# adaLN by row sums on VectorE, one SSD matrix a head, differential norms inside their cores, parameters a phase earlier

## The chip, the cores and the metric

The kernel runs on one core of a Trainium2 chip. The metric is the device time of one execution in microseconds (us). The engines are TensorE (PE, matmuls; PEld its weight loads), VectorE (DVE), ScalarE (ACT), GpSimd (POOL) and SyncE (SP, which issues most DMAs).

## What is computed

One inference step of a hybrid backbone: 2 layers over 128 context and 512 latent tokens of width 1024, all in fp32. The same weights serve both kinds of tokens, with two conditioning vectors (`c_ctx` and `c`). Of each layer:

```python
sh1, sc1, g1, sh2, sc2, g2 = split(silu(cond) @ w_mod[l] + b_mod[l], 6)   # adaLN: parts 0 to 5
h = rmsnorm(x, g_norm1) * (1 + sc1) + sh1
z, xbc, dt, u, dq, dk, dv, wq, wk, wv = split(h @ w_in)
y_a = ssd_mixer(z, xbc, dt)        # bidirectional Mamba-2, chunks of 128, 8 heads of 64
y_b = s5_mixer(u)                  # bidirectional S5
o = (softmax(q1 k1) - lam * softmax(q2 k2)) v      # differential attention, 4 heads
y_c = rmsnorm(o, subln_g) * (1 - lam_init)
y_d = windowed_attention(wq, wk, wv)
merged = sum_i sigmoid(h @ w_gate_i) * (y_i @ w_branch_i) @ w_out
x = x + g1 * merged
h2 = rmsnorm(x, g_norm2) * (1 + sc2) + sh2
x = x + g2 * (relu(h2 @ w_fc1) ** 2 @ w_fc2)
```

Within a chunk and a head the SSD is, for each direction, y = (C B^T * decay, lower or upper triangle) (dt * x); the two directions are added.

## The kernel before

Activations lie feature-major, `[128, 8, 640]`, each as a rounded part and a remainder (`hh`, `hl`; `nh`, `nl`; `fh`, `fl`; `mh`, `ml`). A dense product is three matmuls for each of 8 slices of depth (`mm3_step`, L223 to L225): 24 matmuls of 320 columns make one group in a `dn` tile of PSUM, of which there are two. Weights come with SP's queue (`wr`), ACT rounds them (`wh`, L212), and DVE, every third time POOL, makes the remainder (`wl`, L196), in rings of 4. A group is emptied from PSUM by its evacuation: in the MLP's first half by ACT's Relu and DVE's product `r` (L1746), then ACT's `fh` and the remainder `fl`; in its second half by DVE's multiply-add into `x` (L1538).

The stages, with their times in the profiled execution: prologue (0 to 45), pre (to 195), mix of layer 0 (to 820, its SSD from 445 to 570), end and output projection (to 1042), MLP of layer 0 (1075 to 1595), then the same for layer 1 (SSD from 1905 to 2040, mix to 2270, MLP from 2560).

The order of the mix is written by hand: PLAN is a string of letters, each of which steps one generator (`c` is `ssd_core`, `a` and `A` are `diff_core` for two heads each, `f` is `diff_finish`, `k` the windowed attention, `q` the merge of the differential branch); a table says which must be whole before another begins. A list scheduler then orders the instructions of each engine statically, by priorities; on the chip each engine runs its own list in order.

**adaLN.** A part of the modulation vectors is 1024 numbers for two conditions. `adaln_ahead` makes a quarter of a part a visit: weights in 256 KB tiles `wa` (a ring of 8), 8 matmuls with the condition (L288), ACT copies the row `mrow` out (L293), two matmuls with a selector turn it into columns (L295), DVE adds the bias (`mod`, L298). In layer 0 parts 0 and 1 are made in the prologue; the other 40 visits come ahead of their use: 12 in pre and the output projection, the other 28 in the MLP of layer 0. There `between`, after each two groups, steps one chain of generators 5 times in 8 turns: the rest of adaLN, the builder of layer 1's S5 tables (`s5_build`, its products `cmul` at L593 to L595 on DVE and POOL), adaLN again.

**SSD.** For a chunk and a group g of four heads: `sseg` (the decay's exponents for two directions, DMA, then DVE and POOL subtract, L1022), their minimum (L1026), the exponential (ACT, L1027); `mf` and `ee` are its products with the masked scores `cm` of the two directions (L1033 on POOL, L1034 on DVE); two matmuls a head (L1037, L1038) with `xd`, which is x times the dt of a direction (POOL, L1006). `y` is evacuated by DVE (L1041).

**Differential branch.** `diff_core` leaves raw outputs in the tiles of its queries (`dq` and `BT`) and their sums of squares in `dss`. `diff_finish` computes one `rsqrt` of 128x20 on DVE (L174 to L186), multiplies (L1467), and `to_branch` transposes on PE (L1127) into the tile `B` that the merge's dense groups read (ACT L1131, DVE L1132).

## Time and profile before

| | us |
|---|---|
| median of 3 runs | 2989.94 (2985.88 to 3001.45) |
| profiled execution, its own time | 2994.21 |
| its span | 2992.4 |
| PE busy in the span | 2831.8 (95%) |
| DVE busy | 1686.3 (56%) |
| ACT busy | 1181.3 (39%) |
| POOL busy | 832.8 (28%) |
| mean granted clock of PE | 0.976 |

The chain of work that ended last runs over PE for 72%, DVE for 13%, DMA for 4%, issue for 3%. The share of an engine is an average over stages that differ; what an instruction is worth is read in its own stage, from what waits for it there. Matmuls overlap, so their durations sum to more than the time they take: the distance of two starts is the cost of one.

### The profile page before, as it was taken

The numbers are of one execution on the slowest core, as the hardware profiler recorded it, in microseconds if no ns is written. First come the engines' busy times: TensorE is split into PE (matmuls) and PEld (weight loads), VectorE is DVE, ScalarE is ACT, GpSimd is POOL, SyncE is SP. The second block draws the span as 40 slices with busy tenths as digits, with TensorE's granted clock in tenths as the row PEclk, the third lists the DMA queues.
The fourth block names the chain that finished last, engine by engine and source line by source line (L and its number), as shares of the span: only waits on it lengthen the run. The fifth ranks groups of instructions, "written<-read, shape, count | busy, mean of one in ns | idle before, by whom it ended". The sixth has DMA issues, their size and how long they took to land.

```text
span 2992.4 us, 53739 instructions
## 1 busy us (share of the span) xinstructions
PE 2831.8 (95%) x20782; PEld 2651.5 (89%) x20782; DVE 1686.3 (56%) x3574; ACT 1181.3 (39%) x2692; POOL 832.8 (28%) x823
## 2 busy tenths in 40 slices
PE   7889998999799999999999999989999999999999
PEld 5878988898689888899998989978997999999999
DVE  7859737665543456646235686576665436433333
ACT  4344563253344242323234555424534434332322
POOL 2743106522212222424111220363131131211111
PEclk9989999998899999999999999989999999999999
DMA  6753343234432635434443433432262323222222
GB/s 225 256 174 112 100 136 102 80 99 136 141 100 75 239 103 174 146 114 159 153 144 112 158 100 115 136 92 66 86 198 86 103 89 106 68 75 78 75 75 85
DMA packets 241855, 364.19 MB, mean 122 GB/s; under 512 B 42272, under 2 KB 104480, under 8 KB 241600
## 3 DMA queue, kind: packets, MB, share of 16 engines
q1 hardware_dynamic: 226848, 336.97, 36.0%
q10 hardware_dynamic: 14752, 23.78, 2.2%
q8 instruction: 164, 2.69, 0.4%
q14 instruction: 91, 0.75, 0.1%
HBM read 294.98 MB, written 65.68 MB: 121 GB/s over the span
## 4 chain that ended last, share of the span: by engine, by line
PE 72%; DVE 13%; DMA 4%; issue 3%; ACT 2%; POOL 2%; SPq 0%; DVEq 0%; ACTq 0%; POOLq 0%
PE dn L223 20%; PE dn L224 20%; PE dn L225 20%; DVE wl L196 2%; DMA sseg<-acum 1%; PE mx L288 1%; PE mx L1278 1%; PE pb L1322 1%; PE mx L1407 1%; PE mx L1452 1%; PE mx L1316 1%; DVE B L767 1%; DVE sc L766 1%; PE mx L743 1%; DVE cv L902 1%
## 5 line engine op out<-in xcount | busy, mean ns | idle before, releaser
L196 POOL TENSOR_TENSOR wl<-wr,wh 128x512 fp32r<-128x512 f32 x207 | 287.1, 1387 | 1340.7 <-ACT wh L212 1254.5
L212 ACT CAST wh<-wr 128x512 fp32r<-128x512 f32 (+1 forms) x614 | 377.3, 620 | 600.5 <-PE dn L224 525.1
L196 DVE TENSOR_TENSOR wl<-wr,wh 128x512 fp32r<-128x512 f32 (+1 forms) x407 | 326.4, 805 | 318.1 <-ACT wh L212 306.4
L223 PE MATMUL dn<-hh,wh 128*128 128x320 f32 x1328 | 422.3, 318 | 12.3 <-ACT us L695 3.8
L224 PE MATMUL dn<-hl,wh 128*128 128x320 f32 x1328 | 420.2, 316 | 2.8 <-DVE hl L401 1.5
L225 PE MATMUL dn<-hh,wl 128*128 128x320 f32 x1328 | 418.8, 316 | 1.6 <-DVE wl L196 1.6
L223 PE MATMUL dn<-nh,wh 128*128 128x320 f32 x992 | 311.1, 314 | 6.6 <-DVE r L1746 6.6
L223 PE MATMUL dn<-fh,wh 128*128 128x320 f32 x1008 | 313.6, 311 | 2.9 <-DVE x L1538 2.9
L224 PE MATMUL dn<-nl,wh 128*128 128x320 f32 x992 | 308.5, 311 | 3.9 <-DVE nl L401 1.6
L225 PE MATMUL dn<-fh,wl 128*128 128x320 f32 x1008 | 312.1, 310 | 0.0
L224 PE MATMUL dn<-fl,wh 128*128 128x320 f32 x1008 | 311.8, 309 | 0.0
L225 PE MATMUL dn<-nh,wl 128*128 128x320 f32 x992 | 307.6, 310 | 0.0
L223 PEld LDWEIGHTS dn<-hh,wh 128*128 128x128 f32 x1328 | 253.4, 191 | 19.4 <-ACT us L695 4.1
L223 PE MATMUL dn<-wh,hh 128*128 128x256 f32 (+1 forms) x880 | 259.2, 296 | 8.2 <-DVE dtraw L1207 3.0
L224 PE MATMUL dn<-wl,hh 128*128 128x256 f32 (+1 forms) x880 | 256.8, 293 | 10.5 <-DVE wl L196 8.5
L224 PEld LDWEIGHTS dn<-hl,wh 128*128 128x128 f32 x1328 | 253.3, 191 | 8.3 <-issue 3.2
L225 PEld LDWEIGHTS dn<-hh,wl 128*128 128x128 f32 x1328 | 253.2, 191 | 6.9 <-issue 3.8
L225 PE MATMUL dn<-wh,hl 128*128 128x256 f32 (+1 forms) x880 | 256.0, 292 | 0.0
L1538 DVE SCALAR_TENSOR_TENSOR x<-dn,mod,x 128x192 f32<-128x192 f32 (+2 forms) x240 | 98.0, 436 | 225.2 <-PE dn L225 217.7
L223 PE MATMUL dn<-B,wh 128*128 128x320 f32 x640 | 206.2, 323 | 12.7 <-ACT B L825 3.4
L224 PE MATMUL dn<-B,wh 128*128 128x320 f32 x640 | 202.1, 316 | 0.2 <-DVE B L196 0.2
L225 PE MATMUL dn<-B,wl 128*128 128x320 f32 x640 | 200.4, 313 | 0.0
(399 smaller groups left out, 6505.6 us busy)
## 6 DMA issues: line engine op xcount, KB each, us to landing
wr<-in_w_fc_dram SPq DMA_DIRECT2D x256, 256.0 KB, 2.8
wa<-in_w_mod_dram SPq DMA_DIRECT2D x160, 256.0 KB, 4.5
wr<-in_w_gate_dram SPq DMA_DIRECT2D x128, 256.0 KB, 2.8
wr<-in_w_tok_dram SPq DMA_DIRECT2D x80, 256.0 KB, 2.9
wr<-in_w_branch_dram SPq DMA_DIRECT2D x64, 256.0 KB, 3.0
acc<-gth SPq DMA_DIRECT2D x48, 320.0 KB, 3.1
gold<-acc SPq DMA_DIRECT2D x48, 320.0 KB, 3.7
gate<-gah ACTq DMA_DIRECT2D x70, 160.0 KB, 1.8
```

Of the source, the lines that this page charges most:

```text
L196: engine.tensor_tensor(out=out, in0=full, in1=hi, op=ALU.subtract)
L212: nc.scalar.copy(out=hi, in_=raw)
L223: nc.tensor.matmul(ps, sh, vh, start=first, stop=False)
L224: nc.tensor.matmul(ps, sh, vl, start=False, stop=False)
L225: nc.tensor.matmul(ps, sl, vh, start=False, stop=last)
L288: nc.tensor.matmul(acc[r0:r0 + 32, i * 256:i * 256 + 256], cpad[:, k, :], raw(part, k // 2)[:, c0:c0 + 256], start=(n_ < 4), stop=(n_ >= 4),)
L743: nc.tensor.matmul(xs[:, ri, g * NI:(g + 1) * NI], pm[:, ri, g * 128:(g + 1) * 128], U[:, g0 + g], start=True, stop=True)
L766: nc.vector.tensor_tensor(out=t, in0=v.to_broadcast(shp), in1=x.to_broadcast(shp), op=ALU.mult)
L767: nc.vector.tensor_tensor(out=dst, in0=dst, in1=t, op=ALU.add)
L902: nc.vector.scalar_tensor_tensor(out=cv, in0=xp[:, k:k + 646], scalar=cw[:, f, k:k + 1], in1=cv, op0=ALU.mult, op1=ALU.add)
L1278: nc.tensor.matmul(sc[:, n, c0:c0 + (k1 - k0) * 128], qT[rows[n], g, ct], kT[rows[n], k0:k1].rearrange("p k c -> p (k c)"), start=True, st ...
L1538: nc.vector.scalar_tensor_tensor(out=xs, in0=ps[:, c0:c1], scalar=mods[l][:, part * 8 + f, s:s + 1], in1=xs, op0=ALU.mult, op1=ALU.add)
```

## The change

1. **adaLN in the MLP stages** is made on DVE. The conditioning vectors are spread over all partitions (`cb`), the weights come transposed, 128 outputs x 1024 inputs a tile of 512 KB (`w_modt`, ring of 3), and one instruction multiplies a tile with a condition, sums along the row and adds the bias. One such row op is issued after each evacuation (`fill`). The visits of the first three parts that were still to come for layer 0 stay on PE, ahead of the MLP; the 28 in MLP 0 go. 96 row ops stand in MLP 0 and 16 in MLP 1. The S5 builder is stepped once in six turns. `cmul`'s temporaries have one buffer there instead of two.
2. **SSD**: `md`, the scores of both directions weighted by dt and added (ACT and DVE, a head at a time), is multiplied with the decay once; one matmul a head, on x itself. `xd` and `mf` go.
3. **Differential branch**: each `diff_core` ends with its own `rsqrt` (128x10) and products; `diff_finish` only transposes.
4. **Small parameters** of a layer (`params`) are prepared in the prologue and at the end of the MLP before.
5. The last layer's final squares are left out, as nothing reads them.

The diff, cut to its core:

```diff
-    t1=3, tx=4, tq=6, ty=2, tw=5, td=5, nt=4, wa=8, wr=4, wh=4, wl=4, fh=10,
+    t1=3, tx=4, tq=6, ty=2, tw=5, td=5, nt=4, wa=3, wr=4, wh=4, wl=4, fh=10,
...
-    sub0="v", sub1="p", mf="p", ef="v", xd="p", xw="p", xD="p", off="p", z="v", qkn="p", qka="p", qkc="v",
+    sub0="v", sub1="p", xw="p", xD="p", off="p", z="v", qkn="p", qka="p", qkc="v",
...
-        return ring("wa", 512, "ada" if "ada" in top else "pool")(shape, name)
+        return ring("wa", 1024, "ada" if "ada" in top else "pool")(shape, name)
...
+    cr = tmp([128, 16], "cr", bufs=1)
+    sp.dma_start(out=cr, in_=a["c_rows"])
+    crt = tmp([128, 16], "crt", bufs=1)
+    nc.scalar.activation(out=crt, in_=cr, func=AF.Tanh, scale=0.5)
+    nc.vector.tensor_scalar(out=crt, in0=crt, scalar1=0.5, scalar2=0.5, op0=ALU.mult, op1=ALU.add)
+    nc.vector.tensor_tensor(out=cr, in0=cr, in1=crt, op=ALU.mult)
+    c_d = dp.tile([128, 16], F32, name="c_d")
+    sp.dma_start(out=c_d, in_=cr)
...
-                    if n not in halves:
-                        halves[n] = wa([128, 512], "wa")
-                        sp.dma_start(
-                            out=halves[n], in_=a["w_mod"][l, part * 4 + q, n // 2][:, (n % 2) * 512:(n % 2) * 512 + 512]
-                        )
-                    return halves[n]
+                    if n // 2 not in halves:
+                        halves[n // 2] = wa([128, 1024], "wa")
+                        sp.dma_start(out=halves[n // 2], in_=a["w_mod"][part * 4 + q, n // 2])
+                    return halves[n // 2][:, (n % 2) * 512:(n % 2) * 512 + 512]
...
+    def cond_rows():
+
+        cb = big([128, 2, D], "cb")
+        sp.dma_start(out=cb.rearrange("p s k -> p (s k)"), in_=c_d.rearrange("a b -> (a b)").unsqueeze(0).to_broadcast((128, 2 * D)))
+        return cb
+
+    def adaln_rows(l, parts, cb, after=()):
+
+        for part in parts:
+            for f in range(part * 8, part * 8 + 8):
+                with tc.high_priority(offset=AHEAD):
+                    w = wa([128, D], "wa")
+                    sp.dma_start(out=w, in_=a["w_modt"][l * 48 + f - 40])
+                prod = mx().rearrange("p a b -> p (a b)")
+                for s in range(2):
+                    nc.vector.tensor_tensor_reduce(
+                        out=prod, in0=w, in1=cb()[:, s], scale=1.0, scalar=bmod[l][:, f:f + 1], op0=ALU.mult,
+                        op1=ALU.add, accum_out=mods[l][:, f, s:s + 1],
+                    )
+                    if s and f % 8 == 7 and part in after:
+                        make_gsc(l, after[part])
+                    yield
 
...
-            u, v = big(shape, "s5u", bufs=2, where=where), big(shape, "s5v", bufs=2, where=where)
+            u, v = (big(shape, t, bufs=2 if where == "build" else 1, where=where) for t in ("s5u", "s5v"))
...
-            xd = [times(dt[:, c, 8 * d:8 * d + 8], "sxd") for d in range(2)]
...
+                md = tx([128, 4, 128], "smd")
+                for h in range(4):
+                    n = 4 * g + h
+                    nc.scalar.activation(out=md[:, h], in_=cm[:, 0, g], func=AF.Copy, scale=dt[:, c, n:n + 1])
+                    nc.vector.scalar_tensor_tensor(
+                        out=md[:, h], in0=cm[:, 1, g], scalar=dt[:, c, 8 + n:9 + n], in1=md[:, h], op0=ALU.mult,
+                        op1=ALU.add,
+                    )
...
-                eng("mf").tensor_tensor(out=mf, in0=ee, in1=cm[:, 1, g].unsqueeze(1).to_broadcast(b4), op=ALU.mult)
-                eng("ef").tensor_tensor(out=ee, in0=ee, in1=cm[:, 0, g].unsqueeze(1).to_broadcast(b4), op=ALU.mult)
+                nc.vector.tensor_tensor(out=ee, in0=ee, in1=md, op=ALU.mult)
                 for h in range(4):
                     hc = slice((4 * g + h) * 64, (4 * g + h) * 64 + 64)
-                    nc.tensor.matmul(yp[:, hc], ee[:, h], xd[0][:, hc], start=True, stop=False)
-                    nc.tensor.matmul(yp[:, hc], mf[:, h], xd[1][:, hc], start=False, stop=True)
+                    nc.tensor.matmul(yp[:, hc], ee[:, h], r["xs"][:, c, hc], start=True, stop=True)
             xw = [times(wd[:, d], "sxw") for d in range(2)]
...
-    def diff_core(l, i, qkv, nlam, ss):
+    def diff_core(l, i, qkv, nlam):
+        ss = tmp([128, NT, 2], "dss")
...
-                yield
-
-    def diff_finish(l, outs, ss, gs, var):
-        rs = rsqrt(ss.rearrange("p i t h -> p (i t h)"), NT * 4, 1.0 / 128)
-        rs = rs.rearrange("p (i t h) -> p i t h", i=2, h=2)
+                if (t, h) != (NT - 1, 1):
+                    yield
+        rs = rsqrt(ss.rearrange("p t h -> p (t h)"), NT * 2, 1.0 / 128).rearrange("p (t h) -> p t h", h=2)
+        for t in range(NT):
+            ov = qT[:, :, t * 128:(t + 1) * 128]
+            eng("diff").tensor_tensor(
+                out=ov, in0=ov, in1=rs[:, t].unsqueeze(2).to_broadcast((128, 2, 128)), op=ALU.mult
+            )
+
+    def diff_finish(l, outs, gs, var):
         yo = var["yc"] = branch_tiles()
         for i in range(2):
             for t in range(NT):
                 ct = slice(t * 128, (t + 1) * 128)
-                ov = outs[i][:, :, ct]
-                eng("diff").tensor_tensor(
-                    out=ov, in0=ov, in1=rs[:, i, t].unsqueeze(2).to_broadcast((128, 2, 128)), op=ALU.mult
-                )
-                to_branch(yo, [ov[:, h] for h in range(2)], t, lambda f: gs[:, 0:1], 2 * i)
+                to_branch(yo, [outs[i][:, h, ct] for h in range(2)], t, lambda f: gs[:, 0:1], 2 * i)
                 yield
...
-            nc.vector.scalar_tensor_tensor(
+            ins = nc.vector.scalar_tensor_tensor(
                 out=xs, in0=ps[:, c0:c1], scalar=mods[l][:, part * 8 + f, s:s + 1], in1=xs, op0=ALU.mult, op1=ALU.add
             )
+        return ins
...
+    def params(l):
+
+        bg = tmp([128, 32], "bgh", bufs=1)
+        sp.dma_start(out=bg, in_=a["b_gate"][l])
+        nc.vector.tensor_scalar(out=bg, in0=bg, scalar1=0.5, scalar2=None, op0=ALU.mult)
+        return bg, qk_gains(l), diff_params(l)
...
+        prm = params(0)
         build_after[0] = h[1][0:1, KT - 1, T - 1:T].bitcast(F32)
-        adgen = adaln_ahead(0, range(2, 6), {4: 1})
+        adgen = adaln_ahead(0, (2, 3, 4), {4: 1})
...
+            rows = iter(())
+
+            def fill(ins):
+
+                with tc.issue_after(ins.ins):
+                    step(rows)
+
             def res(part, squares, f, hf, ps):
-                residual(l, part, ps, hf, f, x)
+                ins = residual(l, part, ps, hf, f, x)
                 if squares:
                     square_into(acc_n, x, f, hf)
+                fill(ins)
 
...
-                nc.vector.tensor_tensor(out=r, in0=r, in1=ps, op=ALU.mult)
+                ins = nc.vector.tensor_tensor(out=r, in0=r, in1=ps, op=ALU.mult)
                 hi, lo = hsl(act[j], 0, hf)
                 nc.scalar.copy(out=hi, in_=r)
                 sub_lo(lo, r, hi)
+                fill(ins)
...
-            bgen = [adgen]
+            cb = cond_rows()
+            step(adgen, 99)
+            rows, bgen = adaln_rows(l, (5,), lambda: cb), iter(())
             if l + 1 < L:
-                bgen += [
-                    adaln_ahead(l + 1, (0, 1), {1: 0}),
-                    s5_build(l + 1, "mlp", lambda: act0[7][1][0:1, 0, T - 1:T].bitcast(F32)),
-                    adaln_ahead(l + 1, range(2, 6), {4: 1}),
-                ]
-            bgen = itertools.chain(*bgen)
+                rows = itertools.chain(rows, adaln_rows(l + 1, range(5), lambda: cb, {1: 0, 4: 1}))
...
-                step(bgen, turn * 5 // 8 - (turn - 1) * 5 // 8)
+                step(bgen, int(turn % 6 == 0))
...
-                        res(5, q == 3, f, hf, ps[:, :HF])
+                        res(5, q == 3 and l + 1 < L, f, hf, ps[:, :HF])
...
+            step(rows, 99)
             if l + 1 < L:
+                prm = params(l + 1)
...
+    p["w_modt"] = np.concatenate([inp["w_mod"][0].T.reshape(48, 128, D)[40:], inp["w_mod"][1].T.reshape(48, 128, D)])
```

**DVE in the first MLP stage, where the S5 tables of layer 1 are built.** Names: `r` and `fl` belong to evacuations, `wl` to weights, the `s5` names to the builder; `ISA` on 128x1024 is a row op and on 128x1 the read of its sum. Before:

```order
L593 TENSOR_TENSOR s5u_14611<-s5pin_14078,s5bt_14593 128x512
L1746 TENSOR_TENSOR r_2544_13483<-r_2544_13483,dn_13458 128x320
L595 TENSOR_TENSOR s5bt_14593<-s5u_14600,s5v_14601 128x64
L593 TENSOR_TENSOR s5u_14616<-s5pin_14078,s5bt_14593 128x512
L196 TENSOR_TENSOR fl_13269<-r_2544_13483,fh_13268 128x320
L196 TENSOR_TENSOR wl_13615<-wr_13612,wh_13614 128x512
L1746 TENSOR_TENSOR r_2546_13513<-r_2546_13513,dn_13488 128x320
L595 TENSOR_TENSOR s5pt_14610<-s5u_14611,s5v_14612 128x512
```

In the changed kernel:

```order
L1797 TENSOR_TENSOR r_2586_13595<-r_2586_13595,dn_13570 128x320
L352 ISA mx_13602,mod_102<-wa_13600,cb_12212,bmod_98 128x1024
L352 ISA mod_102 128x1
L626 TENSOR_TENSOR s5pt_13810<-s5u_13816,s5v_13817 128x512
L196 TENSOR_TENSOR wl_13715<-wr_13712,wh_13714 128x512
L196 TENSOR_TENSOR fl_13393<-r_2586_13595,fh_13392 128x320
L624 TENSOR_TENSOR s5u_13838<-s5pou_12802,s5c_13791 128x512
L1797 TENSOR_TENSOR r_2590_13629<-r_2590_13629,dn_13604 128x320
L352 ISA mx_13602,mod_102<-wa_13600,cb_12212,bmod_98 128x1024
```

Each evacuation (`r`, now L1797) is followed by a row op and its read, ahead of the builder's and the weights' operations; the builder's stand further apart.

**PE at the end of the mix of layer 0.** `dn` are dense groups, `pa<-ident,dq` and `pa<-ident,BT` the transposes of the two halves of the differential outputs, L1278 and L1316 (now L1315 and L1353) the windowed attention. Before:

```order
L225 MATMUL dn_8659<-B_7376,wl_8602 128x320
L1278 MATMUL mx_8949<-wkT_1579,xs_7391 128x128 x2
L1127 MATMUL pa_8701<-ident,dq_534_2488 128x128 x2
L1127 MATMUL pa_8709<-ident,dq_534_2488 128x128 x2
L1316 MATMUL mx_8968<-ident,wp_8957 128x128
...
L1127 MATMUL pa_8717<-ident,dq_534_2488 128x128 x2
L223 MATMUL dn_8796<-B_8699,wh_8782 128x320
```

In the changed kernel:

```order
L225 MATMUL dn_8551<-B_7418,wl_8509 128x320
L1164 MATMUL pa_8761<-ident,dq_527_2479 128x128 x2
...
L225 MATMUL dn_8598<-B_7418,wl_8585 128x320
L1164 MATMUL pa_8768<-ident,dq_527_2479 128x128 x2
L223 MATMUL dn_8613<-B_7418,wh_8584 128x320
...
L225 MATMUL dn_8833<-B_8746,wl_8820 128x320
L1164 MATMUL pa_8782<-ident,BT_5979 128x128 x2
L1353 MATMUL mx_9005<-ident,wp_8994 128x128
L1315 MATMUL mx_9014<-wkT_1578,xs_7433 128x128 x2
```

The five transposes of `dq` stood together behind the last dense group of a merge; now each stands alone, with dense groups before and behind it, and the first of `BT` follows dense matmuls too.

**DVE in the SSD of layer 1.** Names as in the section on the kernel; `smd` is `md`. Before:

```order
L1022 TENSOR_TENSOR sseg_20958<-sseg_20958,dac_20919 128x512
L1026 TENSOR_TENSOR sseg_20958<-sseg_20958,sseg_20959 128x512
L1022 TENSOR_TENSOR sseg_20980<-sseg_20980,dac_20919 128x512
L1029 TENSOR_TENSOR swd_20957<-sseg_20958,dtd_20910 128x4 x2
L1022 TENSOR_TENSOR sseg_21214<-sseg_21214,dac_20919 128x512
L196 TENSOR_TENSOR wl_21972<-wr_21969,wh_21971 128x512
L1034 TENSOR_TENSOR sseg_20958<-sseg_20958,scb_20943 128x512
L1026 TENSOR_TENSOR sseg_20980<-sseg_20980,sseg_20981 128x512
```

In the changed kernel:

```order
L1053 SCALAR_TENSOR_TENSOR smd_20949<-scb_20938,dtd_20570,smd_20949 128x128 x3
...
L1053 SCALAR_TENSOR_TENSOR smd_20949<-scb_20938,dtd_20570,smd_20949 128x128
L1061 TENSOR_TENSOR sseg_21059<-sseg_21059,dac_20579 128x512
...
L1072 TENSOR_TENSOR sseg_20958<-sseg_20958,smd_20949 128x512
L1065 TENSOR_TENSOR sseg_21033<-sseg_21033,sseg_21034 128x512
...
L1068 TENSOR_TENSOR swd_21023<-sseg_21033,dtd_20570 128x4 x2
L1072 TENSOR_TENSOR sseg_20984<-sseg_20984,smd_20975 128x512
```

The four multiply-adds of a group stand ahead of the one product (L1034 before, L1072 now) on which PE waits.

## Rows read from the trace of the kernel before

**Rows 1.** Stages: busy us (instructions) of PE, PEld, DVE, ACT, POOL; clock; DMA share.

```profile
445.00:570.00 125.00, 112.52 (x753) 100.32 (x753) 88.82 (x153) 37.83 (x91) 78.23 (x65) 0.93 0.34 97
1075.00:1595.00 520.00, 506.90 (x3910) 471.48 (x3910) 261.50 (x534) 156.04 (x322) 143.64 (x131) 1.00 0.44 143
1905.00:2040.00 135.00, 119.41 (x813) 106.59 (x812) 98.83 (x154) 39.10 (x95) 81.42 (x68) 0.92 0.37 106
2560.00:2992.40 432.40, 428.55 (x2922) 428.28 (x2920) 146.50 (x286) 130.38 (x251) 69.21 (x60) 1.00 0.25 76
```

**Rows 2.** Groups by line, PE, 1075 to 1595: busy, mean, idle before, releaser.

```profile
L288 PE MATMUL mx<-wa,cpad 128*32 128x256 f32 x432 | 33.1, 384 | 2.8 <-DMA wa<-in_w_mod_dram 2.8
...
L295 PE MATMUL mx<-sel,mrow 128*128 128x2 f32 x112 | 14.1, 234 | 0.0
```

**Rows 3.** Timeline of PE around one adaLN visit: start, duration, line, operation.

```profile
1440.67 0.50 PE L295 MATMUL mx<-sel,mrow 128*128 128x2 f32 x4
1441.10 1.07 PE L288 MATMUL mx<-wa,cpad 128*32 128x256 f32 x16
1442.11 0.41 PE L224 MATMUL dn<-fl,wh 128*128 128x320 f32 x1
1442.36 0.31 PE L225 MATMUL dn<-fh,wl 128*128 128x320 f32 x1
```

**Rows 4.** Groups by line and shape over the whole run, DVE and ACT.

```profile
L1291 DVE TENSOR_REDUCE wm<-mx 128x2 f32<-128x1024 f32 x16 | 19.6, 1225 | 41.2 <-PE mx L1285 41.1
...
L1132 DVE SCALAR_TENSOR_TENSOR B<-pa,dgs,B 128x128 fp32r<-128x128 f32 x40 | 13.8, 346 | 6.0 <-ACT B L1131 5.3
...
L1430 ACT ACTIVATION_READ_ACCUMULATOR dp<-mx,dnm 128x1 f32 x80 | 15.7, 197 | 0.0
```

**Rows 5.** Table of 40-us slices of the first MLP stage.

```profile
1280.00:1320.00 40.00, 40.00 (x305) 36.79 (x304) 21.11 (x40) 8.99 (x16) 12.80 (x11) 1.00 0.43 136
...
1360.00:1400.00 40.00, 37.04 (x333) 35.69 (x331) 33.93 (x53) 15.81 (x35) 20.19 (x17) 1.00 0.46 154
```

**Rows 6.** Groups by line: PE in 445:570 and in 1905:2040, POOL in 445:570.

```profile
L1037 PE MATMUL mx<-sxd,sseg 128*128 128x64 f32 x80 | 16.5, 290 | 4.5 <-DVE sseg L1034 4.5
...
L1037 PE MATMUL mx<-sxd,sseg 128*128 128x64 f32 x80 | 16.9, 296 | 5.8 <-DVE ry L186 3.0 <-DVE sseg L1034 2.9
...
L1033 POOL TENSOR_TENSOR sseg<-sseg,scb 128x512 f32<-128x512 f32 x10 | 14.3, 1430 | 9.2 <-ACT sseg L1027 6.7 <-ACT dcl L1021 1.4 <-DMA gate<-gah 1.1
```

**Rows 7.** Timeline in the SSD of layer 0: POOL, DVE, then PE.

```profile
459.85 1.65 POOL L1033 TENSOR_TENSOR sseg<-sseg,scb 128x512 f32<-128x512 f32 x1
...
460.27 1.77 DVE L1022 TENSOR_TENSOR sseg<-sseg,dac 128x512 f32<-128x512 f32 x1
...
462.12 0.68 DVE L1026 TENSOR_TENSOR sseg<-sseg,sseg 128x512 f32<-128x512 f32 x1
...
464.18 0.41 PE L1037 MATMUL mx<-sxd,sseg 128*128 128x64 f32 x2 [0.98 <-DVE sseg L1034]
465.77 0.39 PE L1038 MATMUL mx<-sxd,sseg 128*128 128x64 f32 x2
```

**Rows 8.** Tables of slices: the end of mixing, layer 0 twice, then layer 1.

```profile
765.00:785.00 20.00, 11.51 (x46) 7.42 (x47) 13.69 (x53) 7.43 (x32) 1.67 (x2) 0.51 0.37 122
785.00:800.00 15.00, 11.86 (x71) 7.86 (x69) 9.54 (x31) 7.93 (x28) 0.99 (x2) 0.86 0.00 0
...
2240.00:2280.00 40.00, 36.12 (x254) 29.09 (x255) 26.05 (x79) 22.76 (x74) 6.22 (x6) 1.00 0.22 67
```

**Rows 9.** Timelines of DVE and of PE at 767 to 773.

```profile
767.56 1.76 DVE L1467 TENSOR_TENSOR dq<-dq,ry 128x256 f32<-128x256 f32 x5
...
768.04 0.69 PE L1127 MATMUL pa<-ident,dq 128*128 128x128 f32 x2 [4.67 <-DVE dq L1467]
772.71 0.69 PE L1127 MATMUL pa<-ident,dq 128*128 128x128 f32 x2 [3.98 <-DVE B L1132]
```

**Rows 10.** DMA issues: count, KB each, median us from issue to landing.

```profile
wm<-in_w_mod_dram SPq DMA_DIRECT2D x16, 512.0 KB, 8.4
```

More of the change, by code (lines that the diff above doesn't have):

```diff
@@ L1454, in diff_core @@
                 nc.scalar.activation(
-                    out=pt[:, T:T + 128], in_=po, func=AF.Square, scale=rc[:, 0:1], accum_out=ss[:, i, t, h:h + 1]
+                    out=pt[:, T:T + 128], in_=po, func=AF.Square, scale=rc[:, 0:1], accum_out=ss[:, t, h:h + 1]
                 )
-                yield
-    def diff_finish(l, outs, ss, gs, var):
-        rs = rsqrt(ss.rearrange("p i t h -> p (i t h)"), NT * 4, 1.0 / 128)
-        rs = rs.rearrange("p (i t h) -> p i t h", i=2, h=2)
+                if (t, h) != (NT - 1, 1):
[7 more added lines that the diff above has]
+    def diff_finish(l, outs, gs, var):
         yo = var["yc"] = branch_tiles()
@@ L1575, in panel_adaln @@
                 for i in range(2):
-                    sp.dma_start(out=w[part][i], in_=a["w_mod"][0, part * 4 + q, i])
+                    sp.dma_start(out=w[part][i], in_=a["w_mod"][part * 4 + q, i])
             if soon:
@@ L1621, in hybrid_body @@
             top["pool"] = pool
-            bg = tmp([128, 32], "bgh", bufs=1)
-            sp.dma_start(out=bg, in_=a["b_gate"][l])
-            nc.vector.tensor_scalar(out=bg, in0=bg, scalar1=0.5, scalar2=None, op0=ALU.mult)
+            bg, g, (nlam, gs) = prm
             done, var, sr = {}, {}, {}
@@ L1627, in hybrid_body @@
             y_d = dp.tile([512, 8, NI], F32, name=f"y_d{l}")
-            g = qk_gains(l)
-            nlam, gs = diff_params(l)
-            dss = tmp([128, 2, NT, 2], "dss", bufs=1)
             def glu():
@@ L1651, in hybrid_body @@
                 p=lambda: diff_project(l, 0, h, g, var),
-                a=lambda: diff_core(l, 0, var["qkv", 0], nlam, dss),
+                a=lambda: diff_core(l, 0, var["qkv", 0], nlam),
                 x=lambda: ssd_project(l, h, sr),
@@ L1658, in hybrid_body @@
                 P=lambda: diff_project(l, 1, h, g, var),
-                A=lambda: diff_core(l, 1, var["qkv", 1], nlam, dss),
+                A=lambda: diff_core(l, 1, var["qkv", 1], nlam),
                 z=lambda: ssd_finish(l, sr["xs"], h, var),
@@ L1662, in hybrid_body @@
                 n=lambda: merge(l, 0, h, var["ya"], acc_d, bg, done),
-                f=lambda: diff_finish(l, (var["qkv", 0][0], var["qkv", 1][0]), dss, gs, var),
+                f=lambda: diff_finish(l, (var["qkv", 0][0], var["qkv", 1][0]), gs, var),
                 k=lambda: win_core(l, var["wv"], var["wq"], var["wk"], var),
@@ L1763, in hybrid_body @@
             norm(l, 1, x, acc_n, *h2, PLAN["mid"], tail, head)
-            bgen = [adgen]
+            cb = cond_rows()
+            step(adgen, 99)
+            rows, bgen = adaln_rows(l, (5,), lambda: cb), iter(())
             if l + 1 < L:
-                bgen += [
-                    adaln_ahead(l + 1, (0, 1), {1: 0}),
-                    s5_build(l + 1, "mlp", lambda: act0[7][1][0:1, 0, T - 1:T].bitcast(F32)),
-                    adaln_ahead(l + 1, range(2, 6), {4: 1}),
-                ]
-            bgen = itertools.chain(*bgen)
+                rows = itertools.chain(rows, adaln_rows(l + 1, range(5), lambda: cb, {1: 0, 4: 1}))
+                bgen = s5_build(l + 1, "mlp", lambda: act0[7][1][0:1, 0, T - 1:T].bitcast(F32))
             acc_n = big([128, T], "acc_n")
@@ L1846, in _pack @@
     p["c_t"] = np.stack([_col(inp["c_ctx"]), _col(inp["c"][0])], -1)
+    p["c_rows"] = np.stack([inp["c_ctx"], inp["c"][0]]).reshape(128, 16)
+    w = inp["w_mod"][0].reshape(2, 4, 128, 24, 256)
     p["w_mod"] = st([
-        st([
-            w.reshape(2, 4, 128, 24, 256)[s, :, :, q].transpose(1, 0, 2).reshape(128, 1024) for q in range(24) for s in range(2)
-        ]).reshape(24, 2, 128, 1024) for w in inp["w_mod"]
-    ])
+        w[s, :, :, q].transpose(1, 0, 2).reshape(128, 1024) for q in range(20) for s in range(2)
+    ]).reshape(20, 2, 128, 1024)
+    p["w_modt"] = np.concatenate([inp["w_mod"][0].T.reshape(48, 128, D)[40:], inp["w_mod"][1].T.reshape(48, 128, D)])
     p["b_mod"] = _col(inp["b_mod"])
```

## The prediction

> **What bounds the kernel now.** I read the table of stages first. TensorE (PE) is busy 95% of the span on the page, and in the two MLP stages it runs at the full granted clock: 506.90 of 520 us in the first, 428.55 of 432.4 in the second [rows 1]. Both run the same dense code; the first has 988 more PE instructions (3910 against 2922), of which 432 and 112 are adaLN's [rows 1, 2]. The rest, some 440, build the tables of the next layer's S5 and stay. So in MLP 0 an instruction taken off PE is time, as long as the engines that empty PSUM keep up. VectorE (DVE) is busy only 261.50 of 520 us there [rows 1]. The two stretches with the SSD (445 to 570 and 1905 to 2040) have PE at 112.52 of 125 and 119.41 of 135 and a clock of 0.93 and 0.92, with DVE at 89 and 99 us and POOL at 78 and 81 [rows 1]: there a chain over several engines shares the bound with PE. Last comes the end of layer 0's mixing, where PE from 765 to 785 is busy 11.51 of 20 us at a clock of 0.51 [rows 8].
>
> **Row sums.** Removed from MLP 0 are 27 visits of 16 records at L288 and 28 of 4 records at L295 [rows 2]. What a visit costs is the hole that it leaves in the dense stream, whose matmuls else start 0.147 us apart. Here L295 starts at 1440.67, L288 at 1441.10, the next dense one at 1442.11, and the one behind it 0.25 later instead of 0.147 [rows 3]: 1.44 + 0.10 = 1.54 us for a visit with its L295, 43.1 us for 28. L288 also waited 2.8 us for its weights [rows 2]. Gone: 46 us.
>
> Added to DVE are 96 row ops in MLP 0 (and 16 in MLP 1, where DVE has 146.50 of 432.4 us [rows 1]: nothing). The trace has no such op. The nearest rows are a reduce over 1024 elements of 1225 ns, and the read of an accumulator of 197 ns on ACT [rows 4]; after's order shows two instructions for each row op. I take 1.42 us; 96 x 1.42 = 136 us. DVE then has 261.5 + 136 = 398 of about 487 us, 82%. From below the bound is 1.2 us, the reduce alone, from above 2.85, when the op also waits out a whole POOL op of 1.43 us [rows 6]; I stay at 1.42, since the reduce has the row op's length.
>
> What is queued behind a row op on DVE is the next evacuation, `wl` and the S5 builder's ops. PE takes 24 x 0.147 = 3.5 us for a group of dense matmuls and `dn` has two buffers, so an evacuation that is 1.4 us late is hidden. Where the S5 builder's ops stand between, it isn't always: of the 40-us slices, 1280 to 1320 has DVE 21.11 busy and PE 40.00, 1360 to 1400 has DVE 33.93 and PE 37.04 [rows 5]. With row ops such a load lasts longer: the builder is now stepped once in six turns over the whole stage, and with these durations after's order gives DVE 3.1 to 3.3 us of work for each 3.5 to 3.9 us of PE in some 65 intervals, 250 us in all. At the loss of the slice above (3 of 40 us) that is 19 us; I add 4 for the rest of the stage, so 23 us of stalls. Before there were 520 - 506.9 = 13.1, of which 2.8 are counted above: 12.7 more. Net: -46 + 13 = **-33**. Ends: -46 (stalls stay as they are) and -20 (a loss of 7.5% over all of the stage, 36 us). The rows' weights come as 512 KB a tile, one for two evacuations, the same bytes as before; the ring is a little shallower. DMA share in MLP 0 is 0.44 [rows 1], so I cost that at nothing, and price its failure below (D).
>
> **One SSD matrix a head.** 16 matmuls a chunk become 8. The eight rows of one group of four heads, each one matmul in two records, start from 464.18 to 465.77 [rows 7]: 1.59/7 = 0.227 us apart, and 0.2225 in the rows between. 8 x 5 chunks x 2 layers x 0.2225 = 17.8 us off PE. Off POOL go 10 `mf` of 1430 ns a layer [rows 6] and 10 `xd` of the same size, some 28 us. On DVE come 40 multiply-adds of 128x128, at 346 ns [rows 4] 13.8 us a layer, and on ACT 40 scalings. DVE's `sseg` and `ry` are what PE waited for at L1037, 4.5 us in layer 0 and 5.8 in layer 1 [rows 6]. Against that, DVE ops were stretched while POOL ran: a `sseg` of 1.77 us ended when POOL's `mf` had ended, and the next one of the same size took 0.68 [rows 7]; four of POOL's nine two-input ops a chunk go. The `md` don't hang on the exponential and can run before it; behind it one product is left, without the POOL op in the chain. I take 5 us off the waits: **-23** for both layers. Ends: -12 (of the 27.6 us more on DVE 6 reach PE) and -33 (the 10.3 us of L1037's waits go, and a little clock).
>
> **Differential norms.** In layer 0 a DVE chain (the norm, then ten products, the first five 1.76 us) holds back the first transposes: PE waits 4.67 us for `dq`, then 3.98 on the next link, and the clock falls to 0.51 for 765 to 785 [rows 8, 9]. Idle from 765 to 800 are 8.5 + 3.1 us; the 11.51 busy us at 0.51 are half lost (5.6), and of the 11.86 at 0.86 another 1.7 [rows 8]: 18.9 us. In after's order the five `dq` transposes stand one by one with 20 or more dense matmuls between them, so that stall goes. What is late next are the `BT` ones: between the last product of attention and the first of them stand 43 dense matmuls, 6.3 us, for a norm and 1.76 us of products which took some 9 us before. So 2 to 3 us stay, and the windowed attention's chain behind it, now with more dense matmuls between its links. I take 14 of 18.9. Layer 1's end lost 3.9 us of 40 at full clock [rows 8]; I take 2. **-16**; ends -6 and -23.
>
> **The rest.** The prologue gets one load, one tanh, two small DVE ops and a store on SP's queue ahead of the weights: two issues, up to +1 us. The parameters' preparation had no PE wait behind it, and moves under dense work; if that cover failed it would cost 1 to 2 us. The last layer's squares went beside PE. Together **+1**.
>
> Sum: -33 - 23 - 16 + 1 = -71. The profiled execution took 2994.2 us, 4.3 more than the median of the runs shown, so the result is 2923 by the one and 2919 by the other; I say **2920**.
>
> **Rivals.** (A) DVE becomes the bound of MLP 0. Without row ops it has 261.5 us there, PE has 474: it decides from (474 - 261.5)/96 = 2.2 us a row op. For it: the row op reads two SBUF tensors, and two-input ops of DVE and POOL exclude each other in the trace, 1.77 against 0.68 us [rows 7]. Against it: POOL is busy 144 of 520 us [rows 1], so most row ops meet none. If every one met one: 261.5 + 96 x 2.85 = 535 us, 15 more than now, and the sum is 15 - 38 = -23: 2971. If two in three did, 2.37 us: 489 us and 10 of losses in the chain, 499, -21 - 38: 2935. Say 2950.
> The Trainium skill, page "SBUF — State Buffer", section "SBUF: two separate sides", speaks against the change here: a VectorE op with two SBUF inputs and a GpSimd op that reads SBUF take a shared port pair for their whole duration, and the later one blocks. The rows of 1.77 and 0.68 us agree with it; by that rule, with a collision each time, the time would be rival A's 2971.
>
> (B) The SSD gains nothing: DVE's 13.8 us a layer lie on its chain (`md`, product, `y`), and the matmuls that are left wait as long as those removed took. For it: DVE is at 71 to 73% there [rows 1], and PE's waits name it. Against it: POOL's ops and their collisions go. 2920 + 23 = 2943.
>
> (C) All goes well: stalls stay as before, the waits at L1037 and all of the loss at the end of mixing go: -46 - 33 - 23 + 1 = -101, 2891.
>
> (D) Slower: row ops wait for their weights, with evacuations queued behind them in order. A 512 KB load took 8.4 us at the start, where the queues are full [rows 10], and a tile is used up in 7 to 8 us; with three tiles it is hidden unless loads stand in SP's queue behind others. The other terms give -38, so MLP 0 would have to grow by 38, to 558 us: (558 - 261.5)/96 = 3.1 us a row op, 1.7 of it waiting each time. At 3.6 us it is 607 us, 2994 + 87 - 38 = 3043. The DMA share of 0.44 speaks against.
>
> (E) The change doesn't do what it says at the differential norms: the transposes start earlier and the same stall comes back at `BT`. 2920 + 12 = 2932, inside the forecast's own spread.
>
> **How the numbers follow.** Chances: forecast with E 0.52 (2905 to 2940), A 0.16, B 0.13, C 0.14, D 0.05. The range takes in C's end and most of A: all low ends together give 2891, all high ones -20 - 12 - 6 + 1 = -37, 2957 by the profiled time and 2953 by the median. I set 2888 to 2957; beyond are D and A's upper end. 0.5%, about what a measurement here can tell from no change, is 15 us: 2975 to 3005. Only mixtures of A with B and D reach it. Faster 0.91, same 0.05, slower 0.04.
>
> **What would show it.** In the profile after: MLP 0 near 487 us, no L288 in it, DVE near 80% busy, row ops near 1.2 us with a 0.2 us read; if they are above 2.2, A holds. PE waits on `r`, `x` and `wl` in it between 15 and 30 us. SSD stretches 10 to 13 us shorter each, POOL near 50 us busy there. The waits of 4.67 and 3.98 us on `dq` gone, the clock above 0.85 in the 40 us around the differential transposes. Wrong it would be if evacuations wait for row weights on DVE, or if the SSD's products wait for `smd`.

## The result, and the profile after

The changed kernel takes 2913.7 us (median of 4 runs, 2913.2 to 2917.3) where the kernel before takes 2991.7 (2985.9 to 3001.5): a ratio of 0.9739, 95% interval 0.9711 to 0.9766, or 78 us less. The forecast was 2920, with 2888 to 2957 around it. The profiled execution has a span of 2911.4 us, 81 less than before. The first row below answers to the first of [rows 1], the third to the second, the fourth to the third, the last to the fourth; the second is the end of layer 0's mix, to be held against [rows 8]. Columns as there: stretch, PE, PEld, DVE, ACT, POOL busy, clock, DMA share, GB/s.

```profile
443.00:582.00 139.00, 129.50 (x916) 117.12 (x916) 112.48 (x253) 61.76 (x165) 70.88 (x66) 0.96 0.34 102
735.00:798.00 63.00, 57.07 (x379) 47.98 (x378) 35.43 (x113) 25.56 (x83) 17.81 (x18) 0.92 0.47 154
1025.60:1554.20 528.60, 499.99 (x3555) 480.75 (x3553) 408.90 (x777) 163.47 (x335) 164.10 (x137) 0.98 0.44 140
1845.00:1994.00 149.00, 135.16 (x975) 122.76 (x973) 114.61 (x256) 63.12 (x170) 70.90 (x63) 0.95 0.39 111
2452.50:2911.40 458.90, 451.45 (x3089) 449.09 (x3088) 182.31 (x360) 140.10 (x276) 81.46 (x69) 1.00 0.25 81
```

PE no longer fills the first MLP stage: 28.6 us of 528.6 are idle, and the clock is 0.98 there. DVE rose to 77% of it. POOL's work in the SSD fell by a quarter: from 86.1 to 62.9 us from the 600th to the 800th dense start in layer 0, counted as below.

To place the gain I count PE's dense work. Every kernel here starts 5168 matmuls at L223 (or the line that it has become), so the time from the k-th to another one is the same dense work, whatever lies between. From the timelines of PE, in us:

| from the k-th to the k-th start | before | after | gain |
|---|---|---|---|
| 0 to 600 (pre, first of mix 0) | 410.3 | 404.9 | 5.4 |
| 600 to 1100 (SSD of layer 0 and behind) | 304.6 | 287.7 | 16.9 |
| 1100 to 1600 (end of mix 0, output projection) | 331.9 | 318.3 | 13.6 |
| 1600 to 2600 (MLP 0) | 539.6 | 514.3 | 25.3 |
| 2600 to 3300 (mix 1 with its SSD) | 435.7 | 418.8 | 16.9 |
| 3300 to 4200 (rest of mix 1, output projection) | 499.3 | 497.9 | 1.4 |
| 4200 to the last (MLP 1) | 425.6 | 422.5 | 3.1 |

Each column is one execution. The changed kernel, run once more (f0 below), differs from its column by up to 3.8 us in the first two stretches (291.5 from the 600th to the 1100th start) and by 0.2 or less in the others, so differences of a few us in the first two tell little.

In MLP 0, PE waits as follows (waits of PE, 1025.6 to 1554.2: who for whom, us in total, times, longest):

```profile
PE dn L223 <- DVE r L1797: 15.0, 10, 2.8
PE pb L664 <- DVE s5pt L626: 4.8, 5, 1.6
PE dn L223 <- DVE x L1577: 4.3, 4, 1.3
PE pb L691 <- DVE s5qt L626: 1.1, 1, 1.1
```

In the same view of the kernel before (1075 to 1595) the waits for the evacuations are shorter:

```profile
PE dn L223 <- DVE r L1746: 7.2, 7, 1.4
PE dn L223 <- DVE x L1538: 2.9, 2, 2.2
```

And a wait is there now that the kernel before did not show: PE's transposes of the S5 builder (L664) wait for DVE. DVE is not late because row ops are dear (instructions of line L352: duration min/median/max in ns, first and last start):

```profile
L352 DVE CUSTOM_DVE_ANT_0 mx<-wa,cb,bmod x112: 1272/1284/2262, 1062.0 to 2537.8; 128x1024 f32<-128x1024 f32 x112
L352 DVE DVE_READ_ACCUMULATOR2_ANT mod<- x112: 128/138/144, 1063.2 to 2539.0; 128x1 f32 x112
```

1.28 + 0.14 = 1.42 us for most, and no idle time in front of one. But they are not spread against the builder. Of the slices of 10 us in this stage, those from 1105 to 1275 have DVE busy for 9.7 us or more, all 17; three of them, and one from later:

```profile
1155.00:1165.00 10.00, 7.19 (x49) 6.62 (x47) 9.93 (x11) 2.32 (x5) 8.49 (x6) 1.00 0.46 157
...
1225.00:1235.00 10.00, 7.06 (x47) 6.26 (x45) 9.97 (x19) 1.95 (x5) 3.38 (x4) 1.00 0.40 122
1265.00:1275.00 10.00, 7.64 (x51) 7.13 (x49) 9.77 (x20) 1.86 (x3) 3.63 (x4) 1.00 0.58 203
1375.00:1385.00 10.00, 10.00 (x71) 9.99 (x70) 7.38 (x13) 2.45 (x4) 1.29 (x1) 1.00 0.68 222
```

And late in the stage the builder's matmuls stand between dense ones, one pair at a time (timeline of PE: start, duration, line):

```profile
1429.99 0.41 PE L224 MATMUL dn<-fl,wh 128*128 128x320 f32 x1
1430.33 0.38 PE L691 MATMUL pb<-s5qt,s5bz 128*32 128x112 f32 x2
1430.64 0.41 PE L225 MATMUL dn<-fh,wl 128*128 128x320 f32 x1
...
1442.36 0.47 PE L224 MATMUL dn<-nl,wh 128*128 128x320 f32 x1
1442.63 0.47 PE L225 MATMUL dn<-nh,wl 128*128 128x320 f32 x1
```

A dense matmul and two records of the builder's take 0.65 us, where the dense one alone takes 0.147. This goes on from 1425 to 1439. From 1436.6 the granted clock is at its lower level, 1.2 GHz, for 6.8 us (0.66 over 1435 to 1445), though PE shows no idle time there, and dense matmuls start 0.27 us apart. The clock is also at this level for 3.4 us each from 1235 and from 1314; in the MLP of the kernel before it was not, from 1069 to 1618.

### The profile page after: what moved, and what is told of

Same layout as the page of the kernel before. It is cut to its first block, busy times and chain, and to the rows that moved or that the text cites. A ratio compares the mean times of both kernels' runs of the same rounds, so it can differ in the third digit from the quotient of the medians.

```text
span 2911.4 us, 52387 instructions
## 1 busy us (share of the span) xinstructions
PE 2756.1 (95%) x20062; PEld 2604.5 (89%) x20062; DVE 1817.3 (62%) x3862; ACT 1187.2 (41%) x2729; POOL 799.0 (27%) x783
## 4 chain that ended last, share of the span: by engine, by line
PE 47%; DVE 6%; DMA 1%; issue 1%; ACT 1%; POOL 1%; SPq 0%; ACTq 0%; DVEq 0%; POOLq 0%
PE dn L223 14%; PE dn L224 14%; PE dn L225 14%; DMA sseg<-acum 1%; DVE wl L196 1%; PE mx L1445 1%; PE mx L1315 1%; PE pb L1359 1%; PE mx L1490 1%; PE mx L1353 0%; PE mx L774 0%; DVE mx L352 0%; DVE nh L420 0%; DVE smd L1053 0%; DVE s5u L624 0%
## 5 line engine op out<-in xcount | busy, mean ns | idle before, releaser
L196 POOL TENSOR_TENSOR wl<-wr,wh 128x512 fp32r<-128x512 f32 x207 | 293.8, 1420 | 1299.7 <-ACT wh L212 1249.3
L196 DVE TENSOR_TENSOR wl<-wr,wh 128x512 fp32r<-128x512 f32 (+1 forms) x407 | 314.0, 775 | 241.3 <-ACT wh L212 236.8
L223 PE MATMUL dn<-hh,wh 128*128 128x320 f32 x1328 | 419.9, 316 | 2.8 <-ACT sg L873 0.8
L223 PE MATMUL dn<-nh,wh 128*128 128x320 f32 x992 | 310.9, 314 | 13.2 <-DVE r L1797 12.3
L223 PE MATMUL dn<-fh,wh 128*128 128x320 f32 x1008 | 313.4, 311 | 5.6 <-DVE x L1577 3.4
L223 PE MATMUL dn<-wh,hh 128*128 128x256 f32 (+1 forms) x880 | 258.5, 296 | 5.0 <-ACT hsq L1222 2.3
L223 PEld LDWEIGHTS dn<-hh,wh 128*128 128x128 f32 x1328 | 251.5, 189 | 9.2 <-issue 2.5
L223 PE MATMUL dn<-B,wh 128*128 128x320 f32 x640 | 206.5, 324 | 13.5 <-DVE gth L1556 4.5
L223 PEld LDWEIGHTS dn<-nh,wh 128*128 128x128 f32 x992 | 188.3, 190 | 17.4 <-DVE r L1797 14.5
```

Source lines behind the costliest of these rows:

```text
L196: engine.tensor_tensor(out=out, in0=full, in1=hi, op=ALU.subtract)
L223: nc.tensor.matmul(ps, sh, vh, start=first, stop=False)
```

## The experiments

Theory: each part acts where its instructions are, and what MLP 0 fell short by is DVE, full while row ops and builder meet. Rivals: the parts help each other; row ops are too dear wherever they stand; the SSD's gain is its chain and not its matmuls.

**One part at a time.** e1 has the row sums alone, e2 the SSD, e3 the norms, g4 the parameters; e4 is the changed kernel with adaLN back on PE. Their edits are the pieces of the diff above; e1 has the last layer's squares left out, too.

> The kernel before with the row sums alone (tiles, ring, S5 stepping and the last layer's squares as in the changed kernel). Theory, additive: MLP 0 goes from 551 us (first dense group of the MLP to the first of the next projection) to 528, some 4 us are lost in the output projection of layer 1, where row weights now compete with the loads of x: 18 to 23 us below before, near 2970. By the prediction's own term, -33, it would be 2959. Rival, the gain of the MLP is an interplay with the other parts: less than 10 us below before.

> The kernel before with one SSD matrix a head alone. Theory: 17.8 us of matmuls and some 12 us of waits and half clock go, 30 us below before, near 2962. By the prediction's term, -23, 2969. Rival B (DVE's 27.6 us more eat the gain): less than 8 us below before, 2984 or more.

> The kernel before with the differential norms in their cores alone. Theory: 14 us in layer 0 and 3 in layer 1, near 2975. Rival E (the same stall comes back at the second half's transposes): 2985 or more, with PE waiting there for the products.

> The changed kernel with adaLN back on TensorE; SSD, differential norms and parameters as changed. Theory, additive: 2914 + 20 = 2934 (2930 to 2938); with the prediction's term 2947. Rival, interplay: within 8 us of the changed kernel.

> The kernel before with the small parameters prepared a phase ahead, alone. By the prediction nothing: within 3 us of before. Rival: the three other parts alone give 49 us of the 78, and the changed kernel without row sums is 15 us better than SSD and norms alone, so this part brings 10 us or more, in the first 400 us or after the MLP of layer 0.

| kernel | us | before, beside it | ratio, 95% interval |
|---|---|---|---|
| e1 row sums alone | 2983.5 | 2995.2 | 0.9956 (0.994 to 0.9972) |
| e2 SSD alone | 2972.3 | 2995.2 | 0.9912 (0.9887 to 0.9937) |
| e3 norms alone | 2980.7 | 2995.2 | 0.9945 (0.9927 to 0.9963) |
| g4 parameters alone | 3008.3 | 2996.4 | 1.0034 (1.0019 to 1.005) |
| e4 all but the row sums | 2942.5 | 2995.2 | 0.982 (0.9796 to 0.9845) |

The single parts sum to -12 - 23 - 14 + 12 = -37 us, and all together bring 78: additivity falls. e4 is 26 us above f0 (2917.0, below), between the theory's 20 and the prediction's 33, so its rival falls. e1 with 12 us misses its theory's 18 to 23, though MLP 0 gives what it said. The same count of dense starts shows where (us, gain against before; minus is a loss):

| stretch | e1 | e2 | e3 | g4 | sum | after |
|---|---|---|---|---|---|---|
| 0 to 600 | 2.2 | -0.2 | -3.0 | 0.5 | -0.5 | 5.4 |
| 600 to 1100 | -5.7 | 15.8 | 4.6 | -5.3 | 9.3 | 16.9 |
| 1100 to 1600 | 1.1 | -4.6 | 13.1 | -0.3 | 9.4 | 13.6 |
| 1600 to 2600 | 25.4 | 0.3 | 0.3 | 0.7 | 26.6 | 25.3 |
| 2600 to 3300 | -8.4 | 10.1 | -0.2 | -0.5 | 0.9 | 16.9 |
| 3300 to 4200 | -4.3 | -2.9 | 1.3 | -2.5 | -8.4 | 1.4 |

In MLP 0 the row sums bring the same 25 us alone and in company; e4 has 537.9 there. The norms bring 13.1 in their own stretch, alone and (13.6) in company. What doesn't add lies in the two mixes. e1 edits no instruction of a mix and yet loses 6 us in the first and 13 from the 2600th start to the 4200th. The order in which the list scheduler puts the mix is another one in e1. I wrote down PE's operations from the 100th to the 1600th start by the tiles that they use, neighbours with the same tiles counted once: of 4582 before, 693 have no partner in the same order in e1. The order is the only difference that I found there, but no run changes the order alone, so that it is the cause stays an inference. In the changed kernel 73 of 83 us of gain lie in the four stretches of its main edits, from the 600th to the 3300th start; it is the single parts that lose elsewhere, 37 us being left of 80. So a single part's time carries 5 to 20 us that belong to no edit of it, of which up to 4 us a stretch can be the one execution's own. Rival E falls: in e3 PE's long waits on `dq` are gone and none comes at `BT`. g4 shows that the parameters' gain which I suspected behind e4 isn't there. It is 12 us slower than before, so the "nothing" that it was held against failed, too; what makes it slower is open.

**What a row op costs, and where.** g1 makes every row op twice; f1 ties the S5 builder's steps behind the evacuation at which they are stepped; f2 makes layer 1's last part in MLP 0 too; f3 is f1 and f2; f0 is the changed kernel again.

```diff
 # g1
-                    nc.vector.tensor_tensor_reduce(
+                    for _ in range(2):
+                        nc.vector.tensor_tensor_reduce(
 # f1
-                step(bgen, int(turn % 6 == 0))
+                if turn % 6 == 0:
+                    with tc.issue_after(last[0].ins):
+                        step(bgen)
 # f2
-            rows, bgen = adaln_rows(l, (5,), lambda: cb), iter(())
+            rows, bgen = iter(()), iter(())
...
-                rows = itertools.chain(rows, adaln_rows(l + 1, range(5), lambda: cb, {1: 0, 4: 1}))
+                rows = itertools.chain(adaln_rows(l, (5,), lambda: cb), adaln_rows(l + 1, range(6), lambda: cb, {1: 0, 4: 1}))
```

> The changed kernel with every row op made twice. Theory, DVE decides in MLP 0 from 2.2 us a row op: 96 x 1.6 = 150 us more on DVE, which then has some 555 us where PE has 490, so the stage grows by 45 to 60 us, near 2965. Rival, DVE's slack still covers it: under 15 us.

g1: 2966.1 us, ratio 0.9895 (0.9864 to 0.9925), 49 more than the changed kernel; from the 1600th to the 2600th start 555.1 us instead of 514.3, with DVE busy for 527.4 of them. The stage grows by 41 us, a little under the theory's 45 to 60, and the rest of the 49 lies in the stages behind it. PE waits for evacuations all along (waits of PE, 1040 to 1620), and the row op is no longer than before (1281 ns at the median).

```profile
PE dn L223 <- DVE r L1798: 47.8, 28, 3.5
PE dn L223 <- DVE x L1578: 12.7, 14, 3.0
```

> The changed kernel once more, as the measure for the three beside it: ratio to before near 0.974.

> The changed kernel with the S5 builder's steps tied behind the evacuation at which they are stepped (as the row ops are), so that its blocks are really spread over MLP 0. Theory: the changed kernel's MLP 0 lost its 10 us to a stretch of 170 us in which DVE had row ops and the builder at once and was full; spread, no 10 us have DVE over 95% for long, PE's waits on r, x, s5pt and s5qt fall from 25 us to under 12, and the time falls by 8 us (3 to 15) against the changed kernel. Rival: the row op's length alone makes the waits, wherever the builder stands: within 3 us of the changed kernel, the waits as before.

> The changed kernel with layer 1's last part of adaLN also in MLP 0 (112 row ops there, none and no conditioning load in MLP 1). Theory: the 2.3 us that PE waits for x in layer 1's output projection, with all DMA engines busy there, and the half clock behind it go: 3 to 4 us below the changed kernel; MLP 0 loses at most 2. Rival: the wait is the load of x itself: no difference.

> Both: 11 us below the changed kernel if they add (8 and 3), near 2903.

| kernel | us | before, beside it | ratio, 95% interval | MLP 0 |
|---|---|---|---|---|
| f0 changed kernel | 2917.0 | 2996.0 | 0.9737 (0.9723 to 0.9752) | 514.5 |
| f1 builder spread | 2893.3 | 2996.0 | 0.9666 (0.9645 to 0.9687) | 489.6 |
| f2 last part early | 2915.3 | 2996.0 | 0.973 (0.9715 to 0.9745) | 516.6 |
| f3 both | 2896.7 | 2996.0 | 0.9684 (0.9659 to 0.9708) | 500.7 |

f1 is 24 us faster than the changed kernel and the fastest here; three times what I expected, and a third of it is what I named. DVE is still full from 1105 to 1165, but behind that never for more than 30 us (slices of 10 us with 9.7 us or more). PE's waits (1025.6 to 1530):

```profile
PE dn L223 <- DVE r L1799: 8.9, 11, 1.6
PE pb L664 <- DVE s5pt L626: 4.2, 4, 1.3
PE pb L691 <- DVE s5qt L626: 2.6, 2, 1.6
PE dn L223 <- DVE x L1577: 1.5, 3, 0.7
```

The four kinds fall from 25.2 to 17.2, 8 us; under 12 was expected. The rest is in the holes that the builder's matmuls leave in the dense stream. I measured each as the distance of the dense starts around it, less 0.147. Before, the holes of MLP 0 sum to 85.3 us in 104 places: 39.2 adaLN alone, 26.8 the builder alone, 12.7 with both, 6.7 the norm; longer gaps between dense matmuls add 14.3. After: 46.4 the builder in 64 places, 5.6 the norm, 22.5 the gaps. In f1: 22.9 the builder in 24 places, 6.1 the norm, 20.8 the gaps. So f1 leaves the dense gaps nearly as they were and takes 23.5 us from the builder, 10 of them waits. The clock is in these sums: the 13.7 us that the changed kernel spends at 1.2 GHz in this stage ahead of 1554 are gone in f1, worth some 7 us by an estimate from half speed. The others are the pieces: here one table's matmuls stand together (timeline of PE, f1), 48 records in 1.25 us from dense start to dense start, against 0.65 us for two records when they alternate.

```profile
1166.69 0.31 PE L224 MATMUL dn<-nl,wh 128*128 128x320 f32 x1
1166.93 0.97 PE L691 MATMUL pb<-s5qt,s5bz 128*32 128x112 f32 x32
1167.72 0.23 PE L697 MATMUL pb<-s5c,s5bz 128*32 128x16 f32 x8
1167.78 0.23 PE L697 MATMUL pb<-s5nc,s5bz 128*32 128x16 f32 x8
1167.94 0.41 PE L225 MATMUL dn<-nh,wl 128*128 128x320 f32 x1
```

f2: its mechanism is there. In the output projection of layer 1 (4000th to 4050th start) the changed kernel takes 26.0 us (25.3 in f0), f2 22.0, as before. In the changed kernel's table of slices all DMA engines are busy at that place, with x and row weights at once:

```profile
2395.00:2400.00 5.00, 2.68 (x17) 2.44 (x16) 2.52 (x5) 1.99 (x4) 0.00 (x0) 0.91 1.03 394
2400.00:2405.00 5.00, 5.00 (x28) 5.00 (x28) 0.41 (x2) 0.18 (x1) 0.00 (x0) 0.75 1.03 392
```

But with 16 more row ops MLP 0 is 2.1 us longer in f2 than in f0, and 11.1 us longer in f3 than in f1. So f2 wins 1.7 us, less than the intervals tell apart, and f3 nothing against f1. In f3 most of the loss is clock: MLP 0 has 24 us at 1.2 GHz there and 3.4 in f1, a difference worth some 10 us at half speed.

**What the SSD's gain is made of.** g2 makes each new matmul twice; g3 puts four products a chunk, read by nobody, back on POOL.

```diff
 # g2
-                    nc.tensor.matmul(yp[:, hc], ee[:, h], r["xs"][:, c, hc], start=True, stop=True)
+                    for _ in range(2):
+                        nc.tensor.matmul(yp[:, hc], ee[:, h], r["xs"][:, c, hc], start=True, stop=True)
 # g3
                 nc.vector.tensor_tensor(out=ee, in0=ee, in1=md, op=ALU.mult)
+                nc.gpsimd.tensor_tensor(out=mf, in0=mf, in1=cm[:, 1, g].unsqueeze(1).to_broadcast(b4), op=ALU.mult)
+                nc.gpsimd.tensor_tensor(
+                    out=mf.rearrange("p h e -> p (h e)").rearrange("p (h e) -> p h e", e=64), in0=xv,
+                    in1=dt[:, c, 8 * g:8 * g + 8].unsqueeze(2).to_broadcast(b64), op=ALU.mult,
+                )
```

> The changed kernel with each of the SSD's new matmuls made twice, so as many as before. Theory, the matmuls are time on PE: 80 x 0.2225 = 18 us more, half in each of the two SSD stretches, near 2934. Rival, they hide behind DVE's chain and the gain came from that chain: under 6 us.

> The changed kernel with four 128x512 products a chunk put back on POOL, whose results nothing reads. Theory, taking POOL's ops away is what let DVE carry the 80 multiply-adds: smd's mean (541 ns) and the sseg products grow, 4 to 12 us more in the two SSD stretches. Rival, POOL's load there doesn't matter: within 3 us.

g2: 2946.0 us, ratio 0.9825 (0.98 to 0.985), 29 more than the changed kernel. From the 600th to the 800th start it is 9.5 us longer than f0, from the 3050th to the 3300th 14.2. The matmuls are time on PE, and somewhat more than the 18 us that their distance makes. g3: 2946.3 us, 0.982 (0.9794 to 0.9847), also 29 more: 7.9 and 20.4 in the same two stretches. Both rivals fall, and POOL weighs three times what I gave it. The groups of DVE by line, first of the changed kernel, then of g3, show one way that it takes:

```profile
L1053 DVE SCALAR_TENSOR_TENSOR smd<-scb,dtd,smd 128x128 f32<-128x128 f32 x80 | 39.4, 541 | 0.0
```

```profile
L1053 DVE SCALAR_TENSOR_TENSOR smd<-scb,dtd,smd 128x128 f32<-128x128 f32 x80 | 49.1, 657 | 0.2
```

The median of one is 342 and 346 ns; the mean grows because some take up to 1383 and 1420 ns, and all that took over 400 ns (21 and 31 of 80) ran beside a POOL op. That is 10 us more on DVE; how much of it reaches PE is not shown. PE's idle time grows by some 17 us in the two layers' SSD (600th to 800th and 3100th to 3300th start, against f0), 7 of it at the matmuls for the product, and it spends 24 us more at 1.2 GHz there. How this divides between POOL's load and the order of the mix, which g3 changes too, was not separated.

## Why the prediction was right

**MLP 0, -33: right in kind, 8 us too much.** The removed visits were sized well: 46 forecast, and the holes with adaLN in them sum to 39.2 alone and 12.7 shared. The row op was sized well too: 1.42 forecast, 1.42 at the median, 1.61 with the waits of some (1.47 and 0.14 in this stage). DVE at 82% forecast, 77% measured. What failed is the sentence that the builder "is now stepped once in six turns over the whole stage", and with it that its matmuls "stay". Stepping is not placing: the scheduler drew its operations forward, and the builder's products on DVE run from 1143 to 1376, as they ran from 1156 to 1390 before; tied in f1, they run to 1485. So DVE was full for 170 us, and the builder's holes on PE grew from 26.8 alone and 12.7 shared to 46.4, a term that I had not in the sum. The stalls between dense matmuls rose by 8 where I had 13 for all. With the builder spread as the prediction had assumed, the stage gains 50.0 us (f1), so for that case 33 was too little. Rival A decided in that third of the stage and nowhere else; its sum of DVE's work comes near g1, with two row ops of 1.43 + 0.13 us each time: 261.5 + 96 x 3.12 = 561 us, 555 measured.

By the rule of the Trainium skill that was weighed (page "SBUF — State Buffer", section "SBUF: two separate sides", the shared port pair) a row op that meets a POOL op waits until that op has ended. The trace agrees: of the 96 row ops of MLP 0, 32 start while a POOL op runs, and 28 of these end 1.09 us behind its end, the longest after 2262 ns; four are not held up. The 52 that meet none take at most 1287 ns, so most met none, as the prediction held; the mean of 1471 ns is 0.19 above the median.

**SSD, -23: low, 10 us too little, at its lower end.** Between the 600th and 800th start 139.7 us became 123.7, between the 3100th and 3300th 138.4 became 121.0: 33 us, 30 in f0 (14.4 and 12.9 alone, in e2). The matmuls are in it as forecast (17.8; g2 gives 24 back). The term of 5 us for waits was wrong in place and size: PE's wait at the remaining matmuls for the product on DVE is still there, 10.2 us in both layers, as 10.3 at L1037 in [rows 6], of which 7.4 were for the product (groups of PE by line, 443 to 582 and 1845 to 1994):

```profile
L1075 PE MATMUL mx<-xs,sseg 128*128 128x64 f32 x80 | 11.3, 287 | 4.4 <-DVE sseg L1072 4.4
...
L1075 PE MATMUL mx<-xs,sseg 128*128 128x64 f32 x80 | 11.2, 289 | 5.8 <-DVE sseg L1072 5.8
```

What went is 7 us of other idle time and 14 us at 1.2 GHz, worth another 7. g3 points to the one through whom it went: POOL, whose relief I had set against DVE's 27.6 us only to call it even; the order of the mix may have a share. Rival B falls, since e2 alone gains 23 us.

**Differential norms, -16: right.** e3 gives 14.5 us in all, 13.1 at the end of layer 0's mix and 1.3 in layer 1's. In the changed kernel PE's waits from 735 to 798 are

```profile
PE mx L1353 <- DVE wp L1350: 3.2, 3, 1.7
PE dn L223 <- DVE gth L1556: 2.4, 3, 1.0
```

so the 4.67 and 3.98 us of [rows 9] are gone, the clock is 0.92 over these 63 us, and neither `dq` nor `BT` is waited for: the 2 to 3 us that I left at `BT` did not come, the windowed attention's own chain did.

**The rest, +1.** The parameters I costed at nothing; alone (g4) they come with a loss of 12 us. Its profiled execution is 7 us longer than before, 5.3 of it in the stretch of the SSD, where they have no instruction. The row weights in MLP 1, which I costed at nothing, take 3.3 us (f0; 4.0 in the first run) in the output projection ahead of it, since they are fetched while x is. MLP 1 itself became 3.1 us shorter, and the stretch of the first 600 starts 5.4 us (3.4 in f0), which no term foresaw. The total came out within 7 us since MLP 0 and the SSD missed to opposite sides, by 8 and 10 us; that closeness is luck. Of the signs that the prediction names, MLP 0 near 487 us and POOL near 50 us busy in the SSD did not come.

**D, the slower side,** had nothing for it: a row op never waited for its weights.

## What to carry to other kernels

Work that moves from a full engine to an idle one is worth its holes in the full engine's stream, measured from start to start, and its price is paid where the idle engine was not idle: look at slices of the stage, not at its average. Where a list scheduler decides, stepping a generator later does not place its work later; tie it to an instruction if it has to be spread (24 us here, more than any term was off). An edit tried alone in such a kernel also changes stretches that it does not touch, here by 5 to 20 us and probably through a new order, so compare stretch by stretch of equal work before a part gets the credit.
